# Conv-FFN of a two-layer trunk: the last pair of inner tiles as eight plain block products, and the last weights' loads ahead of the residual's

## The chip, the cores and the metric

The kernel runs on one core of a Trainium2 chip. The metric is the device time of one execution in microseconds (us), lower is better. The kernel before took 2595.81 us as the median of three runs (2591.06 to 2598.98).

The engines are named as in the profile: PE is the matrix engine (TensorE), DVE the vector engine, ACT the scalar engine, POOL the GpSimd engine, and SP the engine that here only issues DMAs. Each works through its own instructions in the order in which they were written.

## The reference, cut to what matters

A residual trunk of two layers (a gated DeltaNet layer and a chunked attention layer) on 1024 tokens of width 1024. Each layer ends in the same kind of feed-forward block, and only that block is changed:

```python
def conv_ffn(xn, w_up, conv_w, conv_b, w_down):
    h = causal_dwconv(xn @ w_up, conv_w) + conv_b      # 1024 x 5632, three taps along the tokens
    gate, val = h[..., :FFN_DIM], h[..., FFN_DIM:]     # FFN_DIM = 2816
    return (jax.nn.silu(gate) * val) @ w_down          # back to 1024 x 1024

h = h + conv_ffn(rmsnorm(h, f_norm[layer]), f_w_up[layer], f_conv[layer], f_conv_b[layer], f_w_down[layer])
```

All matrices are float32, and the last layer is followed by one more RMSNorm.

## The kernel before

`ffn(layer, ...)` (line 1355) makes the block for one layer. The 2816 inner channels are 22 inner tiles of 128 channels (`FP = 22`). Tile j of the gate and tile j of the value belong together: this is a pair j. A pair is a product of a 2 x 2 block matrix of weights with a 2 x 2 block matrix of activations. The block rows of the weights are the gate's 128 channels (operands 11 and 12: inputs 0 to 511 and 512 to 1023) and the value's (21 and 22). The block columns of the activations are the two halves of the tokens (`HALF = 512`).

**Precision.** Every factor is split into a high part and the rest ("hi", "lo"): ACT rounds a copy (`cut_high`, line 1379), and the rest is a subtraction on POOL or DVE (`cut_low`, line 1384). A product of a 128 x 128 weight block with a 128 x 512 activation block is then three matmuls (`triple`, lines 1393 to 1395), and a block product of two 512-deep operands (`product`, line 1509) is four of these, so twelve matmuls of 128x512.

**Seven products instead of eight.** Pairs 1 to 21 are made by a scheme of the Strassen-Winograd kind: seven block products, numbered 1, 7, 6, 5, 2, 4, 3 in the order of the work, on sums and differences of the blocks. The activation sums are made once (`sums`, `X[4]` to `X[7]`); X[5] is the first input half's second token half minus its first. The weight sums are made for every pair on DVE (`left_sum`, line 1444, rows `r<-r,r`), the results are put together on ACT and DVE (`after`, line 1518, tiles `keep`, `keep7`, `gpre`, `vpre`). Pair 0 (`plain`, line 1547) is made with eight plain products. In `after(j, 6)` the sum `keep7` reads the PSUM bank of product 7 before product 4 adds to that bank, so that product 4 waits for DVE there.

**The rest of the pair.** `taps` (line 1476) applies the convolution: its first tap with the bias on ACT (L1485), two more taps on DVE (L1488). Then `silu` on ACT (L1491), `gated` on DVE, and for the last four pairs `hidden` (L1505 on ACT, a subtraction on DVE) splits the result. `w_down` is applied to pairs 0 to 17 in nine groups (`second`, tiles `pd`, `dh`, `eh`), whose results are added up in DRAM by accumulating DMAs from POOL's queue (`send`, L1729, and `send_e`, L1736). The last four pairs go through `tile_of` (layer 1) or `part` (layer 0), tile `pf`, after the last pair. Layer 1's `pf` starts with the residual `res`, loaded by `load_r` (L1872) and transposed by PE.

**Order.** The order of the work is written out: `step` appends a block product to the list `seq`, and `at(i, f, rank)` puts a piece of other work in front of step i. `pos[j, s]` is the place of the s-th product of pair j, and `end` the place of the last one of pair 21. Each engine's order, and SP's order of loads, follows from the order of these calls. For pair 21 there are no group products left between its products, so its seven products follow each other directly.

**Weights' loads.** `load(j, q)` loads operand q of pair j, 256 KB, on SP's queue, under the name `r`. The buffers `r11`, `r21` and `r22` exist twice, `r12` once, so that the load of pair 21's operand 12 waits until that of pair 20 is read. `load_last(q)` (L1779, L1784, tile `fr`) loads the eight pieces of `w_down` for the last four pairs, and `cut_last` splits them (L1790, tiles `fh`, `fl`).

Of the kernel before, what the change touches and what calls it, by code (L numbers as in the profile page):

```python
# [9 lines left out]
F32 = mybir.dt.float32  # L10
# [6 lines left out]
P = 128  # L17
SEQ = 1024
KT = 8
HALF = 512  # L20
NH_A = 8
NH_B = 16
FP = 22
# [5 lines left out]
def trunk_kernel(  # L29
# [1325 lines left out]
    def ffn(layer, h, hp, xs, tail, d_r, last):  # L1355
# [19 lines left out]
        def at(i, f, rank=1):  # L1375

            jobs.setdefault(max(i, 0), []).append((rank, f))
# [9 lines left out]
        def cut(src, ring, copy=nc.scalar.copy):  # L1387
            hi, lo = cut_high(src, ring, copy)
            cut_low(src, hi, lo, nc.gpsimd)
            return hi, lo  # L1390

        def triple(ps, w, x, cw, first, last):
            mm(ps, w[0][:, cw], x[0], start=first, stop=False, skip_group_check=True)  # L1393
            mm(ps, w[0][:, cw], x[1], start=False, stop=False, skip_group_check=True)  # L1394
            mm(ps, w[1][:, cw], x[0], start=False, stop=last, skip_group_check=True)  # L1395
# [80 lines left out]
        def taps(j, v, step, c0=0, c1=SEQ):  # L1476
            w, m = cf[:, layer, FP * v + j, :], FP * v + j
            if (j, v) not in conv_t:
                if v == 0:
                    conv_t[j, v] = tp.tile([P, SEQ], F32, name="gate", tag="gate")  # L1480
                else:
                    conv_t[j, v] = hp.tile([P, SEQ], F32, name="val", tag=f"h{layer + 1}_{j % 4}")
            t_, p_ = conv_t[j, v], pre[j, v]
            if step == 0:
                nc.scalar.activation(t_[:, c0:c1], p_[:, c0:c1], AF.Identity, scale=w[:, 2:3], bias=cfb[:, layer, m : m + 1])  # L1485
            else:
                a = max(c0, step)
                nc.vector.scalar_tensor_tensor(t_[:, a:c1], p_[:, a - step : c1 - step], w[:, 2 - step : 3 - step], t_[:, a:c1], op0=ALU.mult, op1=ALU.add)  # L1488

        def silu(j, c0=0, c1=SEQ):  # L1490
            nc.scalar.activation(conv_t[j, 0][:, c0:c1], conv_t[j, 0][:, c0:c1], AF.Silu)  # L1491

        def gated(j, c0=0, c1=SEQ):
            tt(nc.vector, conv_t[j, 1][:, c0:c1], conv_t[j, 1][:, c0:c1], conv_t[j, 0][:, c0:c1], ALU.mult)

        def hidden(j, c0=0, c1=SEQ):

            if j not in hid:
                if j == FP - 1:
                    hid[j] = [fin.tile([P, SEQ], F32R, name=f"hid{i}", tag=f"hid{i}") for i in "hl"]  # L1500
                else:
                    room_ = {18: (5, 6), 19: (7, 2), 20: (3, 4)}[j]
                    hid[j] = [hp.tile([P, SEQ], F32R, name=f"hid{i}", tag=f"h{layer + 1}_{n}") for n, i in zip(room_, "hl")]
            (hh, hl), v_ = hid[j], conv_t[j, 1]
            nc.scalar.copy(hh[:, c0:c1], v_[:, c0:c1])  # L1505
            tt(nc.vector, hl[:, c0:c1], v_[:, c0:c1], hh[:, c0:c1].bitcast(F32), sub)
# [11 lines left out]
        def after(j, n):  # L1518
            p_ = bank[j, {2: 1, 4: 7, 3: 5}.get(n, n)]
            if n == 1:  # L1520
                keep[j] = tp.tile([P, HALF], F32, name="keep", tag="keep", bufs=2)
                nc.scalar.copy(keep[j], p_)
            elif n == 6:
                tt(nc.vector, keep[j], p_, keep[j], add)
                keep[j, 7] = tp.tile([P, HALF], F32, name="keep7", tag="keep7")
                tt(nc.vector, keep[j, 7], bank[j, 7], keep[j], add)
            elif n == 5:
                tt(nc.vector, new_pre(j, 1)[:, HALF:SEQ], p_, keep[j, 7], add)
            elif n == 2:
                nc.scalar.copy(new_pre(j, 0)[:, 0:HALF], p_)  # L1530
            elif n == 4:
                tt(nc.vector, new_pre(j, 1)[:, 0:HALF], p_, keep[j], add)
            elif n == 3:
                tt(nc.vector, new_pre(j, 0)[:, HALF:SEQ], p_, keep[j], add)

        pos = {}
        ORDER = 1, 2, 5, 3, 6, 7, 4

# [40 lines left out]
        end, fin_at = pos[FP - 1, 7], pos["d", NG - 1, 4]  # L1579
        early = pos["p", 1, 3]  # L1580
        for i, (j, n) in due.items():
            if i < early:
                low = []
                at(i - 2, lambda j=j, n=n, low=low: low.append(operand(j, n, False)), 1)
                at(i - 2, lambda low=low: low[0](), 2.5)
            else:
                at(i - 2, lambda j=j, n=n: operand(j, n), 1)
                if j > 3 and n in (6, 4):
                    at(i - 2, lambda j=j, n=n: left_sum(j, n - 1), 1.05)
            if n != 2 or j > 2:  # L1590
                at(i + 1, lambda j=j, n=n: after(j, n), 0)

        def nx(j, s):
            return pos[j + 1, s] if j + 1 < FP else end + s
# [43 lines left out]


        def half(c0, c1):  # L1640
            return (
                lambda: (taps(FP - 1, 1, 0, c0, c1), taps(FP - 1, 1, 1, c0, c1), taps(FP - 1, 1, 2, c0, c1), taps(FP - 1, 0, 0, c0, c1), taps(FP - 1, 0, 1, c0, c1)),
                lambda: (taps(FP - 1, 0, 2, c0, c1), silu(FP - 1, c0, c1), gated(FP - 1, c0, c1), hidden(FP - 1, c0, c1)),
            )

        def open_fin():
            nonlocal fin
# [116 lines left out]
        k0 = 2 * NG  # L1764
        fw, fh, fps, norms = {}, {}, {}, []
        n0 = len(seq)
        slots = [(k, 1) for k in range(4)] + [(k, 1) for k in range(4, 8)] if layer == 0 else [(k, 0) for k in range(4)] + [(k, 1) for k in range(4)]
        last_at = [pos[FP - 1, s] for s in (3, 4, 5, 6)] + [end + 1] * 4
        if layer == 1:
            last_at = [pos[FP - 1, 2]] + last_at[:-1]  # L1770
            last_at[5] = end
            last_at[7] = end + 2

        def load_last(q):
            tag = ("a11", "a12", "r11", "r21", "r22", "r11", "r22", "r21")[q]
# [16 lines left out]
            fw[q] = hi, lo  # L1792

        for q in range(8):
            s = (1, 1, 2, 3, 4, 4, 5, 6)[q]
            at(fin_at + 1 if q < 2 else pos[FP - 1, s], lambda q=q: load_last(q), 1)
            at(last_at[q], lambda q=q: cut_last(q), 1.5)

        if layer == 0:
# [55 lines left out]
        else:  # L1855
# [645 lines left out]
```

## Time and profile before

| | |
|---|---|
| median of three runs | 2595.81 us (2591.06 to 2598.98) |
| the profiled execution: its own time | 2593.14 us |
| its span, first to last instruction | 2591.4 us |
| mean granted TensorE clock over the span | 0.992 |
| PE busy / DVE / POOL / ACT | 2513.5 / 1856.7 / 1494.1 / 1410.0 us |
| the seven products of pair 21, layer 0 | 1269.34 to 1293.94, 24.60 us |
| the seven products of pair 21, layer 1 | 2505.37 to 2533.05, 27.68 us |

A row of the timeline gives the start in us from the span's start, the duration, the engine, the line of the code, the operation, output and inputs, and shapes; in brackets stands the idle time just before it and who ended it. "PEclk" is the share of the full TensorE clock that was granted. In the table of stretches each engine's busy time stands in the order PE, PEld (PE's weight loads), DVE, ACT, POOL, and behind them PEclk, the busy share of the DMA engines, and GB/s.

### The profile page before, as it was taken

The page shows a single profiled execution, that of the slowest core. Times are in us where ns is not written, and L with a number is a line of the kernel's source. Part 1 is how long each engine was busy: PE and PEld are TensorE (multiplying, and loading weights), DVE is VectorE, ACT ScalarE, POOL GpSimd, SP SyncE. Part 2 cuts the span into 40 slices and gives each one's busy share as a digit, 9 for nine tenths or more (in the row PEclk, how much of TensorE's full clock was granted, in tenths as well). Part 3 has the DMA queues.
Part 4 walks back from the last instruction along what each step waited for, and adds up shares of the span by engine and source line. Part 5 has one row for each costly group of instructions (what it writes and reads, how often), then busy time and mean ns, then how long its engine had stood idle before and what let it go on. Part 6 is the DMA issues. An engine that isn't in the chain of part 4 may idle for free. (4 is left out here: it accounts for less than half of the span.)

```text
span 2591.4 us, 39359 instructions
## 1 busy us (share of the span) xinstructions
PE 2513.5 (97%) x13933; PEld 2078.2 (80%) x13933; DVE 1856.7 (72%) x3102; ACT 1410.0 (54%) x2708; POOL 1494.1 (58%) x1517
## 2 busy tenths in 40 slices
PE   7999999999999999999999999999999999999998
PEld 5878888888777888888778888887876788888877
DVE  5765775454588888888876666666478788888875
ACT  6444555464455656565455556655345556565543
POOL 3655554345447777777735444444443777777771
PEclk9999999999999999999999999999999999999999
DMA  4534345455336777777841111212332577777785
GB/s 128 138 99 121 116 117 164 134 178 169 96 85 143 146 148 154 153 145 153 186 145 48 47 52 57 73 37 73 133 104 78 134 150 143 154 154 153 154 194 175
DMA packets 317061, 325.93 MB, mean 126 GB/s; under 512 B 32832, under 2 KB 240960, under 8 KB 316864
## 3 DMA queue, kind: packets, MB, share of 16 engines
q1 hardware_dynamic: 285728, 219.33, 28.6%
q0 software_dynamic: 26240, 95.43, 20.6%
q10 hardware_dynamic: 4896, 8.65, 0.9%
q8 instruction: 110, 1.80, 0.3%
q14 instruction: 87, 0.71, 0.1%
HBM read 180.68 MB, written 142.67 MB: 125 GB/s over the span
## 5 line engine op out<-in xcount | busy, mean ns | idle before, releaser
L1360 POOL TENSOR_TENSOR ul<-r,uh 128x512 fp32r<-128x512 f32 x282 | 445.6, 1599 | 295.2 <-ACT uh L1381 273.9
L120 PE MATMUL acc<-xh,whi 128*128 128x512 f32 x896 | 375.5, 420 | 0.3 <-ACT xh L1099 0.2
L105 POOL TENSOR_TENSOR wlo<-wraw,whi 128x256 fp32r<-128x256 f32 (+3 forms) x338 | 248.8, 767 | 206.0 <-ACT whi L103 178.1
L122 PE MATMUL acc<-xh,wlo 128*128 128x512 f32 x896 | 353.3, 394 | 4.2 <-POOL wlo L105 4.2
L121 PE MATMUL acc<-xl,whi 128*128 128x512 f32 x896 | 353.4, 394 | 1.3 <-DVE xl L1100 0.8
L1381 ACT CAST uh<-r 128x512 fp32r<-128x512 f32 x296 | 181.7, 623 | 219.8 <-DVE r L1360 175.2
L1395 PE MATMUL pu<-xh,ul 128*128 128x512 f32 x552 | 217.3, 394 | 3.3 <-POOL ul L1360 3.2
L1393 PE MATMUL pu<-xh,uh 128*128 128x512 f32 x552 | 216.7, 393 | 2.9 <-ACT uh L1381 1.4
L1394 PE MATMUL pu<-xl,uh 128*128 128x512 f32 x552 | 216.3, 392 | 1.0 <-POOL xl L381 1.0
L2125 POOL TENSOR_SCALAR sS<-sS,st 128x640 f32<-128x640 f32 (+4 forms) x128 | 86.4, 680 | 206.5 <-DVE st L2123 197.6
L122 PEld LDWEIGHTS acc<-xh,wlo 128*128 128x128 f32 x896 | 168.8, 188 | 42.6 <-POOL wlo L105 5.3
L1714 ACT COPY stage<-pd 128x1024 f32<-128x1024 f32 x180 | 174.8, 1013 | 49.4 <-PE pd L1395 49.4
L121 PEld LDWEIGHTS acc<-xl,whi 128*128 128x128 f32 x896 | 170.0, 190 | 27.8 <-DVE xl L1100 3.1
L120 PEld LDWEIGHTS acc<-xh,whi 128*128 128x128 f32 x896 | 169.7, 189 | 24.5 <-ACT xh L1099 1.2
L1488 DVE SCALAR_TENSOR_TENSOR val<-vpre,colt,val 128x1023 f32<-128x1023 f32 (+2 forms) x92 | 153.6, 1670 | 38.6 <-ACT val L1485 38.4
L2114 DVE CUSTOM_DVE_ANT_0 sS<-sc,bt 128x640 f32<-128x640 f32 (+4 forms) x128 | 84.1, 657 | 132.5 <-PE sc L2110 87.1
L1360 POOL TENSOR_TENSOR dl<-a,dh 128x512 fp32r<-128x512 f32 x90 | 154.8, 1720 | 38.4 <-ACT dh L1381 38.4
L1488 DVE SCALAR_TENSOR_TENSOR gate<-gpre,colt,gate 128x1023 f32<-128x1023 f32 (+2 forms) x92 | 175.4, 1906 | 0.8
L1360 DVE TENSOR_TENSOR r<-r,r 128x512 f32<-128x512 f32 x168 | 131.6, 783 | 31.1 <-POOL ul L1360 29.7
L1395 PEld LDWEIGHTS pu<-xh,ul 128*128 128x128 f32 x552 | 104.3, 189 | 28.0 <-POOL ul L1360 6.6
L1393 PEld LDWEIGHTS pu<-xh,uh 128*128 128x128 f32 x552 | 104.3, 189 | 25.3 <-ACT uh L1381 1.8
L2183 ACT CAST pTh<-ptp 128x512 fp32r<-128x512 f32 (+2 forms) x176 | 75.4, 452 | 89.7 <-PE ptp L2170 86.3
(390 smaller groups left out, 7125.9 us busy)
## 6 DMA issues: line engine op xcount, KB each, us to landing
r<-in_f_w_up_dram SPq DMA_DIRECT2D x172, 256.0 KB, 4.2
d_r<-stage POOLq DMA_DIRECT2D x78, 512.0 KB, 7.9
d_c<-stage POOLq DMA_DIRECT2D x70, 512.0 KB, 7.9
a<-in_f_w_down_dram SPq DMA_DIRECT2D x72, 256.0 KB, 2.8
wraw<-in_a_w_in_dram SPq DMA_DIRECT2D x32, 512.0 KB, 4.7
d_e<-stage POOLq DMA_DIRECT2D x32, 512.0 KB, 9.1
wraw<-in_a_w_out_dram SPq DMA_DIRECT2D x16, 512.0 KB, 4.3
d_r<-h ACTq DMA_DIRECT2D x32, 256.0 KB, 3.6
```

Of the source, the lines that this page charges most:

```text
L105: nc.gpsimd.tensor_tensor(lo[:, c], raw[:, c], hi[:, c].bitcast(F32), op=ALU.subtract)
L120: mm(ps, hi[:, kw, wcol : wcol + P], rh[k][s], start=st, stop=False)
L121: mm(ps, hi[:, kw, wcol : wcol + P], rl[k][s], start=False, stop=False)
L122: mm(ps, lo[:, kw, wcol : wcol + P], rh[k][s], start=False, stop=sp)
L1360: tt = lambda eng, o, a, b, op: eng.tensor_tensor(o, a, b, op=op)
L1381: copy(hi, src)
L1393: mm(ps, w[0][:, cw], x[0], start=first, stop=False, skip_group_check=True)
L1394: mm(ps, w[0][:, cw], x[1], start=False, stop=False, skip_group_check=True)
L1395: mm(ps, w[1][:, cw], x[0], start=False, stop=last, skip_group_check=True)
L1488: nc.vector.scalar_tensor_tensor(t_[:, a:c1], p_[:, a - step : c1 - step], w[:, 2 - step : 3 - step], t_[:, a:c1], op0=ALU.mult, op1=ALU.add)
L1714: nc.scalar.copy(t_, ps)
L2125: nc.gpsimd.tensor_scalar(S, S, st[:, 3:4], 1.0, op0=ALU.mult, op1=ALU.mult)
```

## The change

Pair 21, the last one, is made with eight plain block products and no weight sums. With A1, A2 the two weight blocks of the value (then of the gate), the first token half is A1·X[1] + A2·X[2]. The second token half is A1·X[5] + A2·X[3] plus a copy (`keep`) of A1·X[1], since X[5] is the difference of the two halves. So the products are 21·X1, 21·X5, 22·X2, 22·X3 for the value, then 11·X1, 11·X5, 12·X2, 12·X3 for the gate. Each operand is cut once and used in two products that follow each other. An ACT copy of the bank after the first product (`keep`, L1550 after the change) must be done before the third product adds to the same bank.

The value is finished after the fourth product, so its taps now run in one piece beside the gate's products; the gate is still finished in two halves. The loads of the last weights move ahead by some steps (`load_last`), and in layer 1 the first four tiles' residual loads move back by two steps each (`load_r`); in layer 1 the split pieces of the last weights are also put into other buffers (`slots`, `last_at`).

```diff
+        def plain_operand(q):
+            ops[FP - 1, q] = cut(raw[FP - 1, q], "u")
+
+        def plain_product(q, n):
+            key = "last", q > 20, n in (3, 5)
+            if n in (1, 5):
+                bank[key] = pacc.tile([P, HALF], F32, name="pul", tag="u", bufs=4)
+            for k in range(4):
+                triple(bank[key], ops[FP - 1, q], X[n][k], kc[k], n in (1, 5) and k == 0, n in (2, 3) and k == 3)
+
+        def plain_after(q, n):
+            v, j = q > 20, FP - 1
+            if n == 1:
+                keep[v] = tp.tile([P, HALF], F32, name="keep", tag="keep", bufs=2)
+                nc.scalar.copy(keep[v], bank["last", v, False])
+            elif n == 2:
+                nc.scalar.copy(new_pre(j, int(v))[:, 0:HALF], bank["last", v, False])
+            elif n == 3:
+                tt(nc.vector, new_pre(j, int(v))[:, HALF:SEQ], bank["last", v, True], keep[v], add)
...
-        plan = first + [(j, n) for j in range(3, FP) for n in (1, 7, 6, 5, 2, 4, 3) if (j, n) != (3, 1)]
+        plan = first + [(j, n) for j in range(3, FP - 1) for n in (1, 7, 6, 5, 2, 4, 3) if (j, n) != (3, 1)]
...
+        closing_pair = [(q, n) for v in (20, 10) for q, n in ((v + 1, 1), (v + 1, 5), (v + 2, 2), (v + 2, 3))]
+        for i, (q, n) in enumerate(closing_pair):
+            pos[FP - 1, i + 1] = len(seq)
+            step((FP - 1, q, n), lambda q=q, n=n: plain_product(q, n))
+        pc = [pos[FP - 1, i + 1] for i in range(8)]
...
+        for i, (q, n) in zip(pc, closing_pair):
+            if n in (1, 2):
+                at(i - 2, lambda q=q: plain_operand(q), 1)
+            at(i + 1, lambda q=q, n=n: plain_after(q, n), 0)
...
-        at(end, half(0, HALF)[0], 2)
-        at(end + 1, half(0, HALF)[1], 2)
-        at(end + 2, lambda: (half(HALF, SEQ)[0](), half(HALF, SEQ)[1]()), 2)
+        at(pc[4], lambda: (taps(j_, 1, 0), taps(j_, 1, 1)), 2)
+        at(pc[5], lambda: taps(j_, 1, 2), 2)
+        at(end, lambda: half(0, HALF), 2)
+        at(end + 1, lambda: half(HALF, SEQ), 2)
...
-            s = (1, 1, 2, 3, 4, 4, 5, 6)[q]
-            at(fin_at + 1 if q < 2 else pos[FP - 1, s], lambda q=q: load_last(q), 1)
+            i = (fin_at + 1, fin_at + 1, pos[FP - 2, 6], pos[FP - 2, 7], pc[0], pc[3], pc[1], pc[1])[q]
+            at(i, lambda q=q: load_last(q), 1)
...
-                at(fin_at + 3 + t if t < 4 else end + 1, lambda t=t: load_r(t), 3.5)
+                at(pc[t] if t < 4 else end + 1, lambda t=t: load_r(t), 3.5)
```

What this moves is seen in the built programs. First SP's queue in layer 1, around the load of pair 21's operand 12 (`r_24631` before, `r_24618` after); `stage` is a total that is read back, `res` the residual, `fr` the last weights. Before:

```order
L1733 DMA stage<-d_e_1_19578 128x1024
L1872 DMA res<-d_r_97 128x4x128
L1872 DMA res<-d_r_99 128x4x128
L1439 DMA r_24631<-in_f_w_up_dram 128x4x128
L1872 DMA res<-d_r_97 128x4x128
L1872 DMA res<-d_r_99 128x4x128
```

After the change:

```order
L1766 DMA stage<-d_e_1_19570 128x1024
L1813 DMA fr<-in_f_w_down_dram 128x512 x2
L1439 DMA r_24618<-in_f_w_up_dram 128x4x128
L1813 DMA fr<-in_f_w_down_dram 128x512
L1901 DMA res<-d_r_97 128x4x128
L1901 DMA res<-d_r_99 128x4x128
```

Two loads still stand ahead of the operand's, but they are last weights and no longer residual.

Then the same place in layer 0, where there is no residual to load. Before:

```order
L1733 DMA stage<-d_e_1_7524 128x1024
L1439 DMA r_12572<-in_f_w_up_dram 128x4x128
L1779 DMA fr<-in_f_w_down_dram 128x4x128 x6
L1843 DMA h_12755<-d_r_89 128x512
L1843 DMA h_12756<-d_r_89 128x512
```

After the change:

```order
L1766 DMA stage<-d_e_1_7524 128x1024
L1808 DMA fr<-in_f_w_down_dram 128x4x128 x2
L1439 DMA r_12571<-in_f_w_up_dram 128x4x128
L1808 DMA fr<-in_f_w_down_dram 128x4x128 x4
L1872 DMA h_12757<-d_r_89 128x512
```

In layer 0 operand 12 was next after the total, and now two last weights' loads of 256 KB stand ahead of it.

Last ACT in layer 1, beside the gate's products; `gate<-gate` is pair 20's silu, `uh` the high part of an operand. Before, from the cut of the operand for pair 21's product 2 on (`r_24631`):

```order
L1381 CAST uh<-r_24631 128x512
L1790 CAST fh_24717<-fr 128x512
L1505 CAST hidh<-val 128x1024
L1381 CAST uh<-r_24560 128x512
L1790 CAST fh_24751<-fr 128x512
L1491 ACTIVATE gate<-gate 128x1024
```

After the change, from the copy of the value's first half on:

```order
L1552 COPY vpre<-pul 128x512
L1819 CAST fh_24729<-fr 128x512
L1491 ACTIVATE gate<-gate 128x1024
L1381 CAST uh<-r_24618 128x512
L1485 ACTIVATE val<-vpre,colt 128x1024
L1550 COPY keep<-pul 128x512
```

Operand 12's cut now stands behind pair 20's silu, and the copy `keep`, for which the seventh product waits, stands behind that cut and the value's first tap.

More of the change, by code (lines that the diff above doesn't have):

```diff
@@ L1578, in ffn @@
                         step(("d", g, n), lambda g=g, n=n: second(g, n))
-        end, fin_at = pos[FP - 1, 7], pos["d", NG - 1, 4]
+        closing_pair = [(q, n) for v in (20, 10) for q, n in ((v + 1, 1), (v + 1, 5), (v + 2, 2), (v + 2, 3))]
[3 more added lines that the diff above has]
+        pc = [pos[FP - 1, i + 1] for i in range(8)]
+        end, fin_at = pc[7], pos["d", NG - 1, 4]
         early = pos["p", 1, 3]
@@ L1591, in ffn @@
                 at(i + 1, lambda j=j, n=n: after(j, n), 0)
+        j_ = FP - 1
+        for i, (q, n) in zip(pc, closing_pair):
+            if n in (1, 2):
+                at(i - 2, lambda q=q: plain_operand(q), 1)
+            at(i + 1, lambda q=q, n=n: plain_after(q, n), 0)
         def nx(j, s):
@@ L1640, in half @@
         def half(c0, c1):
[L1641 to L1644, printed above, removed]
+            for i in range(3):
+                taps(j_, 0, i, c0, c1)
+            silu(j_, c0, c1)
+            gated(j_, c0, c1)
+            hidden(j_, c0, c1)
         def open_fin():
@@ L1766, in ffn @@
         n0 = len(seq)
[L1767 to L1772, printed above, removed]
+        slots = [(k, 1) for k in range(4)] + [(k, 1) for k in range(4, 8)] if layer == 0 else [(k, 1) for k in range(4)] + [(k, 0) for k in range(4)]
+        last_at = pc[:4] + ([end + 1] * 4 if layer == 0 else [pc[5], pc[6], end, end + 1])
         def load_last(q):
```

## The prediction

> **What bounds the kernel now.** I read the page's busy times first, then the stretches of pair 21 in both layers, then PE's timeline inside them, then the chain of waits that leads to each idle time there.
>
> ```profile
> PE 2513.5 (97%) x13933; PEld 2078.2 (80%) x13933; DVE 1856.7 (72%) x3102; ACT 1410.0 (54%) x2708; POOL 1494.1 (58%) x1517
> ```
>
> PE is busy for 97% of the span, so elsewhere one more matmul costs its own time and work taken off DVE, ACT or POOL brings nothing. The change is at pair 21, so the question is whether that holds there.
>
> ```profile
> 1269.34:1293.94 24.60, 21.21 (x85) 16.75 (x84) 20.99 (x17) 11.69 (x17) 13.61 (x9) 0.93 0.81 195
> 2505.37:2533.05 27.68, 23.32 (x86) 17.65 (x85) 22.39 (x19) 13.00 (x20) 14.54 (x10) 0.88 0.95 247
> 2533.05:2584.77 51.72, 51.72 (x257) 42.19 (x255) 30.15 (x50) 18.71 (x35) 1.73 (x2) 1.00 0.53 174
> ...
> 1287.55:1290.96 3.41, 3.41 (x9) 2.62 (x8) 2.75 (x3) 1.92 (x4) 2.70 (x2) 0.50 0.78 195
> 2519.76:2523.17 3.41, 3.23 (x8) 2.56 (x9) 3.14 (x2) 1.38 (x3) 3.41 (x3) 0.50 1.12 329
> ```
>
> It does not: in the first two stretches, the seven products of pair 21 in layers 0 and 1, PE has idle time and less than the full clock (PEclk 0.93 and 0.88), while DVE is nearly full. In the third, the last stage of layer 1, PE never stops. The last two rows are pieces of the first two in which the clock was granted at one half. PE's timeline shows the causes; first layer 0, the first matmul of the products 1, 5, 2, 4 and 3 and of the next stage (`pf`):
>
> ```profile
> 1269.34 0.39 PE L1393 MATMUL pu<-xh,uh 128*128 128x512 f32 x1
> ...
> 1277.50 0.39 PE L1393 MATMUL pu<-xt1h,uh 128*128 128x512 f32 x1
> 1280.54 0.39 PE L1393 MATMUL pu<-xh,uh 128*128 128x512 f32 x1
> 1286.78 0.47 PE L1393 MATMUL pu<-xt4h,uh 128*128 128x512 f32 x1 [3.36 <-DVE keep L1360]
> 1291.20 0.39 PE L1393 MATMUL pu<-xh,uh 128*128 128x512 f32 x1
> 1293.94 0.39 PE L1393 MATMUL pf<-hidh,fh 128*128 128x512 f32 x1
> ```
>
> The first three products take 8.16 us, so 2.72 each, with no wait. Seven would be 19.04; the stretch is 24.60, an excess of 5.56: 0.32 in the fourth product, 3.52 in the fifth up to the end of the wait for `keep7` (3.36 idle), 1.70 in the sixth, which runs at half clock right behind that wait, 0.02 in the last. Layer 1:
>
> ```profile
> 2505.37 0.39 PE L1393 MATMUL pu<-xh,uh 128*128 128x512 f32 x1
> ...
> 2510.81 0.39 PE L1393 MATMUL pu<-xt2h,uh 128*128 128x512 f32 x1
> 2511.85 0.50 PE L1395 MATMUL pu<-xt2h,ul 128*128 128x512 f32 x1 [0.42 <-POOL ul L1360]
> 2514.29 0.39 PE L1393 MATMUL pu<-xt1h,uh 128*128 128x512 f32 x1
> 2518.58 0.50 PE L1393 MATMUL pu<-xh,uh 128*128 128x512 f32 x1 [1.41 <-ACT uh L1381]
> 2519.94 0.79 PE L1395 MATMUL pu<-xh,ul 128*128 128x512 f32 x1 [0.62 <-POOL ul L1360]
> 2525.89 0.47 PE L1393 MATMUL pu<-xt4h,uh 128*128 128x512 f32 x1 [1.90 <-DVE keep L1360]
> 2533.05 0.60 PE L1886 MATMUL pf<-ident,res 128*128 128x128 f32 x4
> ```
>
> Here the excess over 19.04 is 8.64: 0.76 in the third product (a wait for POOL), 1.57 in the fourth and 4.59 in the fifth (three waits, 3.93 idle, and some 2 at half clock), 1.72 in the last two at half clock. The chain of waits of layer 1 says what was late:
>
> ```profile
> 2501.76 16.05 DMA r<-in_f_w_up_dram
> 2518.44 0.62 ACT fh L1790
> ...
> 2520.03 2.17 DVE hidl L1360
> ...
> 2524.42 0.61 DVE keep L1360
> ```
>
> The load of operand 12, which product 2 needs as fifth, takes 16.05 us; ACT stands still for it, and with ACT DVE's queue, down to `keep7`. In layer 0 DVE alone is late with `keep7`.
>
> **The change part by part.** *The eighth product* costs 2.72 us of PE in each layer, 5.44 together, on the path. *The waits for `keep7`* go, since no product adds to a bank that DVE still has to read. *Operand 12* is needed as the seventh product, 16.32 us after the start of the first instead of 10.88 plus waits, so layer 1's wait for it goes, with its half clock. With no wait the eight products take 21.76 in either layer.
>
> *The wait in the third product of layer 1* I keep:
>
> ```profile
> 2509.60 0.87 POOL L1736 DMA_DIRECT2D d_c<-stage  x1 [3.30 <-DMA d_c<-stage]
> 2510.21 1.59 POOL L1360 TENSOR_TENSOR ul<-r,uh 128x512 fp32r<-128x512 f32 x1
> ```
>
> POOL issues an accumulating DMA that waits 3.30 us for an earlier one, and the low part of the third product's operand stands behind it. After the change operand 22 stands there. Bounds 0 and 0.76; I take 0.76, as nothing moves that DMA.
>
> So layer 0 gains 24.60 - 21.76 = 2.84, layer 1 gains 27.68 - 21.76 - 0.76 = 5.16.
>
> *DVE, ACT and POOL* lose three operand cuts, three weight sums and the two `keep` sums per layer, which counts only through the waits above. What is added there is the copy `keep` on ACT: the seventh product waits for it. Its queue, by rows of layer 0:
>
> ```profile
> 1271.88 1.41 DVE L1360 TENSOR_TENSOR r<-r,r 128x512 f32<-128x512 f32 x2
> 1274.26 1.47 DVE L1360 TENSOR_TENSOR hidl<-val,hidh 128x1024 fp32r<-128x1024 f32 x1 [0.97 <-ACT hidh L1505]
> ...
> 1279.09 1.78 DVE L1360 TENSOR_TENSOR fl<-fr,fh 128x512 fp32r<-128x512 f32 x1
> ...
> 1283.03 2.28 DVE L1488 SCALAR_TENSOR_TENSOR gate<-gpre,colt,gate 128x1022 f32<-128x1022 f32 x1
> ```
>
> ```profile
> 1268.80 1.24 ACT L1485 ACTIVATE val<-vpre,colt 128x1024 f32<-128x1024 f32 x1
> 1275.28 0.57 ACT L1522 COPY keep<-pu 128x512 f32<-128x512 f32 x1
> 1278.77 0.62 ACT L1790 CAST fh<-fr 128x512 fp32r<-128x512 f32 x1
> 1285.41 1.06 ACT L1491 ACTIVATE gate<-gate 128x1024 f32<-128x1024 f32 x1 [6.02 <-DVE gate L1488]
> ```
>
> On ACT stand ahead of the copy pair 20's silu (1.06), the cut of operand 12 (0.62, as the other casts), the value's first tap (1.24) and the copy itself (0.57), some 3.2 with their overlap. The seventh product starts at 1269.34 + 16.32 = 1285.66, so DVE's last tap of pair 20's gate must end by about 1282.4. Before it ended at 1285.3. Ahead of it go two sums (1.41), the idle 0.97, and about 1.2 at the queue's head (one more sum and a cast that ACT had to make first); one cut of last weights (0.7 to 1.78) comes in; and POOL has one subtraction less beside it, where each one lengthens a tap from 1.3 to 2.3. That gives 1281.2 to 1282.3: in time, by 0.1 to 1.2. I take no wait; the other end, with POOL's help left out, is 1 us late.
>
> *The loads.* In layer 1 two loads of 256 KB stand ahead of operand 12's as before, so by the 16.05 it lands no later than 2517.8; the cut must start by 2505.37 + 16.32 - 2.2 = 2519.5. In layer 0 it was the first in the queue and becomes the third:
>
> ```profile
> 1265.53 0.37 SPq L1439 DMA_DIRECT2D r<-in_f_w_up_dram  x1
> ...
> r<-in_f_w_up_dram SPq DMA_DIRECT2D x1, 256.0 KB, 10.0
> ...
> fr<-in_f_w_down_dram SPq DMA_DIRECT2D x2, 256.0 KB, 15.5
> fr<-in_f_w_down_dram SPq DMA_DIRECT2D x1, 256.0 KB, 2.8
> ...
> 2517.83 1.20 SPq L1872 DMA_DIRECT2D res<-d_r  x2
> ```
>
> As first it took 10.0 us and landed at 1275.6. The second and third there, issued within two microseconds behind it, took 15.5, so landed by about 1282.2; a single one issued once the accumulating DMAs were over took 2.8. Third place is thus 1282.2, and the cut may start as late as 1285.66 - 2.2 = 1283.4. Bounds 1275.6 and, at 10.0 for each of the three, 1295.5; I take 1282.2, the row of that very place in the queue, so no cost. The residual's first four tiles in layer 1 are issued two steps, 5.4 us, later. The last pair of these loads was issued at 2517.83 (the last row), so now at about 2523.3; at the 2.8 of a free queue it lands at 2526, and the transposes behind the last product need the first tile from 2527.9 on and this fourth one last. I cost that at nothing: the last products cover it, and without them it would cost its lateness, one for one.
>
> *The end of each layer* has less behind the last product than before, as the value is finished by then; before it hid under the next stage's matmuls, 51.72 busy of 51.72 in layer 1. No cost, no gain. In layer 0 one wait stands further down:
>
> ```profile
> 1332.25 1.05 PE L372 MATMUL pss<-ones,nacc 128*128 128x2 f32 x8 [1.43 <-DVE nacc L369]
> ```
>
> It is the norm behind the block, late on DVE. With less DVE work ahead it may go, or stay: 0 to 1.43, I take 0.7.
>
> The sum: 2.84 + 5.16 + 0.7 = 8.7 us. Against the profiled execution's own 2593.14 (span 2591.4) that is 2584.4; its run lies 2.7 below the median of 2595.81, from which it would be 2587.1. I take 2586, between the two.
>
> **The rivals.** *The half clock does not hang on these waits.* For it: layer 1's idle times are short, 1.41, 0.62 and 1.90, and yet a window is 3.41 long (2519.76 to 2523.17). Then 1.70 in layer 0 and about 3.7 in layer 1 stay: a gain of 3.3, 2591.4. Against it: each half-clock window begins inside or right behind a wait, and the stretch with PE busy without a break has PEclk 1.00. The Trainium skill, "TensorE: Matmul & The Clock Gate", section "Why this matters for your kernels", holds that the clock falls back after an idle window and warns of gaps over some 3 us between matmuls. By that rule layer 0's 3.36 would do it and layer 1's gaps would not, so that only layer 1's 3.7 would stay, 2589.7. This trace speaks against so long a threshold: 0.50 was granted around waits of under 2 us.
>
> *The copy `keep` is late.* Each layer where it is 2 us late pays 2 and 1.7 of half clock: 2589.7 with one, 2593.4 with both. For it: a margin of 0.1 to 1.2 on DVE and 1.2 on the load.
>
> *The other side: operand 12 of layer 0 stuck behind the last weights.* At 10.0 us for each load it lands at 1295.5, PE waits 12.1 at the seventh product and runs 1.7 longer behind it: 2586 + 13.8 = 2599.8, slower than before. It turns the gain into a loss from a landing at about 1290.4 on. Against it: third place took 15.5 us, not 30.
>
> **How the numbers follow.** The forecast has 0.60, the late copy 0.22 (mostly one layer), the half clock that stays 0.10, the stuck operand 0.08. A measurement of this kernel tells about 0.3%, 7.8 us, from no change. The forecast's 8.7 lies little above: of its 0.60 I put 0.52 beyond 7.8, plus 0.10 from the late copy where it is only tenths late and layer 1's third wait goes too. Faster 0.62. The rest of the rivals on this side is within 0.3%, 0.32; of the stuck operand 0.06 is slower by more. The range: at the low end every wait gone, the third product's and the norm's too (8.76 + 1.43 = 10.2, from 2593.14: 2583), and 3 us for the spread of the runs; at the high end the copy late in both layers. 2580 to 2593.5.
>
> **What would show it.** Right: the eight products take 21.8 in layer 0 and 21.8 to 22.5 in layer 1, PEclk 1.00 in both, no wait for `keep`, and operand 12 of layer 0 landing near 1282 and cut in time. Wrong: a wait of the seventh product's first matmul for ACT `keep`, or ACT standing before the cut of operand 12 for a DMA, with a half-clock window behind it; or half clock without a wait.

## The result and the profile after

The changed kernel took 2583.89 us (median of 7 runs, 2581.55 to 2590.04), the kernel before beside it 2594.50 (median of 7): a ratio of 0.9967, 95% interval 0.9955 to 0.9980, so about 8.6 us less. The profiled execution of the changed kernel has a span of 2582.2, that of before 2591.4.

The page's line of busy times, and then the windows of the changed kernel: pair 21 of layer 0, pair 21 of layer 1, and the last stage of layer 1. Columns are length, then busy time (and instructions) of PE, PEld, DVE, ACT and POOL, PEclk, DMA share, GB/s.

```profile
PE 2510.3 (97%) x13957; PEld 2076.1 (80%) x13957; DVE 1845.4 (71%) x3084; ACT 1409.3 (55%) x2704; POOL 1483.3 (57%) x1511
```

```profile
1270.95:1293.12 22.17, 22.11 (x97) 17.94 (x96) 20.24 (x16) 12.42 (x17) 7.85 (x6) 1.00 0.89 219
2501.32:2523.79 22.47, 22.32 (x98) 17.82 (x97) 20.51 (x16) 13.59 (x20) 9.22 (x7) 1.00 1.09 277
2523.79:2575.51 51.72, 51.72 (x257) 42.17 (x255) 26.80 (x46) 16.44 (x32) 1.29 (x1) 1.00 0.55 184
```

Eight products take 22.17 and 22.47 us where seven took 24.60 and 27.68, at full clock (1.00, before 0.93 and 0.88); PE is busy in 22.11 and 22.32 of them. The last stage is the same 51.72. PE's timeline shows the starts of the first and seventh product and of the next stage in layer 0, the same three in layer 1, and the norm's matmul behind layer 0:

```profile
1270.95 0.39 PE L1393 MATMUL pul<-xh,uh 128*128 128x512 f32 x1
...
1287.55 0.50 PE L1393 MATMUL pul<-xh,uh 128*128 128x512 f32 x1
...
1293.12 0.39 PE L1393 MATMUL pf<-hidh,fh 128*128 128x512 f32 x1
...
1330.63 1.05 PE L372 MATMUL pss<-ones,nacc 128*128 128x2 f32 x8 [0.63 <-DVE nacc L369]
...
2501.32 0.39 PE L1393 MATMUL pul<-xh,uh 128*128 128x512 f32 x1
...
2518.20 0.50 PE L1393 MATMUL pul<-xh,uh 128*128 128x512 f32 x1
...
2523.78 0.38 PE L1915 MATMUL pf<-ident,res 128*128 128x128 f32 x2
```

The seventh product starts 16.60 us behind the first in layer 0 and 16.88 in layer 1; six products without a wait are 16.32. What holds it is in the waits of layer 1's stretch, where PEld is the weight load ahead of a matmul:

```profile
POOL d_c L1769 <- DMA d_c<-stage: 4.4, 1, 4.4
...
PEld pul L1393 <- ACT keep L1550: 0.6, 1, 0.6
PEld pul L1395 <- POOL ul L1360: 0.4, 1, 0.4
```

The copy `keep` is a little late, and so is GpSimd's low part of operand 22, for the third product, which stands behind an accumulating DMA. The norm's wait fell from 1.43 to 0.63. Together: 24.60 - 22.17 = 2.43, 27.68 - 22.47 = 5.21, and 0.80, which makes 8.44 of the profiled span's 9.2. The other 0.8 is the rest of larger differences in stretches that the change does not touch: this execution comes to pair 21 of layer 0 1.61 us later than that of before, and takes 2.43 us less from the norm to pair 21 of layer 1, where one window ran at half clock and before five.

### The profile page after: what moved, and what is told of

The parts are those of the page before. It is cut to its first block, busy times and chain, and to the rows that moved or that the text cites. A ratio compares the mean times of both kernels' runs of the same rounds, so it can differ in the third digit from the quotient of the medians.

```text
span 2582.2 us, 39356 instructions
## 1 busy us (share of the span) xinstructions
PE 2510.3 (97%) x13957; PEld 2076.1 (80%) x13957; DVE 1845.4 (71%) x3084; ACT 1409.3 (55%) x2704; POOL 1483.3 (57%) x1511
## 5 line engine op out<-in xcount | busy, mean ns | idle before, releaser
L1360 POOL TENSOR_TENSOR ul<-r,uh 128x512 fp32r<-128x512 f32 x276 | 437.4, 1605 | 286.4 <-ACT uh L1381 265.2
L1395 PE MATMUL pu<-xh,ul 128*128 128x512 f32 x528 | 207.0, 392 | 2.7 <-POOL ul L1360 2.6
L1393 PE MATMUL pu<-xh,uh 128*128 128x512 f32 x528 | 206.6, 391 | 1.4 <-DVE h L1261 0.9
L1394 PE MATMUL pu<-xl,uh 128*128 128x512 f32 x528 | 206.4, 391 | 1.0 <-POOL xl L381 1.0
L1488 DVE SCALAR_TENSOR_TENSOR val<-vpre,colt,val 128x1023 f32<-128x1023 f32 x88 | 152.9, 1738 | 35.6 <-ACT val L1485 35.6
L1360 DVE TENSOR_TENSOR r<-r,r 128x512 f32<-128x512 f32 x160 | 126.3, 789 | 31.1 <-POOL ul L1360 29.7
L1360 DVE TENSOR_TENSOR el<-val,eh 128x512 fp32r<-128x512 f32 x90 | 86.3, 959 | 46.0 <-ACT eh L1381 46.0
```

The lines of the kernel that those rows point to most:

```text
L1360: tt = lambda eng, o, a, b, op: eng.tensor_tensor(o, a, b, op=op)
```

## Experiments

**The changed kernel once more**, beside the next three.

> The changed kernel itself, to compare the others with on the same chip: about 2584 us, 8 to 10 less than the kernel before, stretches of 22.2 and 22.5 us.

2585.45 us beside 2591.32, ratio 0.9973 (0.9962 to 0.9985), somewhat less than the 8 to 10 us expected; its stretches are 22.46 and 23.28. In layer 1 the third product waits 1.22 us for GpSimd here, so that wait differs from execution to execution. Against the same profile of before, the two stretches of this execution gain 2.14 and 4.40 us.

**Products without the loads' order.** The cuts of the first last weights go back with their loads.

```diff
-        last_at = pc[:4] + ([end + 1] * 4 if layer == 0 else [pc[5], pc[6], end, end + 1])
+        last_at = [pc[2], pc[3], pc[4], pc[5]] + [end + 1] * 4 if layer == 0 else [pc[1], pc[2], pc[3], pc[4], pc[5], end, end + 1, end + 2]
...
-            i = (fin_at + 1, fin_at + 1, pos[FP - 2, 6], pos[FP - 2, 7], pc[0], pc[3], pc[1], pc[1])[q]
+            i = (fin_at + 1, fin_at + 1, pc[1], pc[2], pc[3], pc[3], pc[4], pc[5])[q]
...
-                at(pc[t] if t < 4 else end + 1, lambda t=t: load_r(t), 3.5)
+                at(fin_at + 3 + t if t < 4 else end + 1, lambda t=t: load_r(t), 3.5)
```

> The eight plain products stand, but the loads of the last weights, the cuts they feed and the first loads of the residual are issued where they were before the change. Theory one: the gain comes from the products, because the accumulating product no longer waits for the two sums keep and keep7, and the order of the loads carries nothing. Then layer 0 takes 21.8 to 22.4 us in the eight products, layer 1 22.0 to 23.0, the clock stays at 1.00, and the whole is within 2 us of the changed kernel (about 2584). Rival: layer 1 needs the loads' order too. Then the last weights come in behind the residual's tiles, ScalarE stands still for them ahead of the copy keep, and layer 1 takes 25 us or more, with half clock behind a wait: about 2587.

2589.87 us, ratio 0.9991 (0.9982 to 1.0000): nearly all the gain is gone. The windows of both stretches, then from the timelines of layer 1 PE's seventh product, ScalarE's cut of the third last weight, SyncE's loads, and SyncE's own waits at the residual's:

```profile
1266.40:1288.16 21.76, 21.76 (x98) 18.02 (x96) 18.78 (x16) 12.54 (x17) 9.50 (x6) 1.00 0.94 230
2497.70:2527.30 29.60, 24.72 (x98) 19.64 (x97) 20.53 (x16) 13.45 (x19) 9.24 (x7) 0.88 1.07 307
```

```profile
2519.31 0.80 PE L1393 MATMUL pul<-xh,uh 128*128 128x512 f32 x1 [4.88 <-ACT keep L1550]
...
2514.62 0.62 ACT L1819 CAST fh<-fr 128x512 fp32r<-128x512 f32 x1 [7.68 <-DMA fr<-in_f_w_down_dram]
...
2494.47 12.77 SPq L1901 DMA_DIRECT2D res<-d_r  x4
2507.29 2.63 SPq L1813 DMA_DIRECT2D fr<-in_f_w_down_dram  x1
...
SPq L1901 <- PE pul L1395: 6.9, 2, 6.6
```

In layer 0 the products alone do it all: 21.76, eight times 2.72 without a wait. In layer 1 they are worse than before, 29.60 against 27.68. SyncE stands 12.77 us at four of the residual's loads, 6.9 of it until PE has read the buffers that they fill; the last weight's load comes behind them, ScalarE waits 7.68 us for it, and the copy `keep`, further back on ScalarE, keeps PE waiting 4.88. The first theory is wrong for layer 1, the rival right.

**The loads' order without the products**, on the kernel before.

```diff
-            s = (1, 1, 2, 3, 4, 4, 5, 6)[q]
-            at(fin_at + 1 if q < 2 else pos[FP - 1, s], lambda q=q: load_last(q), 1)
+            i = (fin_at + 1, fin_at + 1, pos[FP - 2, 6], pos[FP - 2, 7], pos[FP - 1, 1], pos[FP - 1, 4], pos[FP - 1, 5], pos[FP - 1, 6])[q]
+            at(i, lambda q=q: load_last(q), 1)
...
-                at(fin_at + 3 + t if t < 4 else end + 1, lambda t=t: load_r(t), 3.5)
+                at(pos[FP - 1, t + 1] if t < 4 else end + 1, lambda t=t: load_r(t), 3.5)
```

> The kernel before, seven products with their sums, with only the loads issued in the new order (last weights ahead of the residual's first tiles; two of the last weights stay where they were, since their rooms are still in use). Theory one: nothing is gained. Layer 0 stays at 24.6 us (its waits are on VectorE's queue), layer 1 at 26.5 to 28, the whole within 2 us of the kernel before. Rival: the order of the loads is what took layer 1's waits away. Then layer 1 falls to 24.5 us or less and the whole by 3 us or more.

2596.94 us, ratio 1.0018 (1.0009 to 1.0027): slower. The windows, and a wait in layer 0:

```profile
1270.83:1297.83 27.00, 21.96 (x86) 16.52 (x84) 20.07 (x17) 11.78 (x17) 13.62 (x9) 0.94 0.69 166
2509.35:2536.62 27.27, 23.40 (x85) 17.58 (x84) 22.39 (x19) 12.94 (x20) 14.58 (x10) 0.87 1.02 252
```

```profile
ACT uh L1381 <- DMA r<-in_f_w_up_dram: 5.5, 1, 5.5
```

Layer 0 loses 2.40, because operand 12, now third in the queue, is still needed as fifth and ScalarE waits 5.5 us for it; layer 1 gains 0.41. The theory had layer 0 unmoved and missed that; that the loads alone bring no gain holds. The parts don't add: in layer 1 the products alone cost 1.92, the loads alone bring 0.41, and both together bring 5.21.

**Which load it is in layer 1.** Once the products without the loads' order, but with the residual at the changed places, and once the changed kernel with only the residual at the old places (each is the last pair of lines of the first diff, one way or the other).

> The eight products with the last weights' loads and cuts at the old places, as in products_alone, but the residual's first four tiles loaded at the changed kernel's places, each one or two products later. In products_alone SyncE stood 12.77 us at the residual's third to sixth load, and the last weights' third load, issued behind them at 2507.29, kept ScalarE 7.68 us. Theory: that stand is the cause, so with the residual behind the third load ScalarE's wait falls under 3 us, keep is late by less than 2 us, and layer 1 takes 22.0 to 25 us, not 29.60. Rival: the last weights' own late places are the cause; then ScalarE still waits some 7 us for the third load and layer 1 stays at 28 us or more. Layer 0 has no residual loads and stays at 21.8 to 22.2 by both.

> The changed kernel with only the residual's first four tiles loaded at the old places. The last weights' third and fourth load are now issued ahead of the residual's load at which SyncE stands. Theory: what matters is that these two are not behind that stand, so the residual's place alone does nothing: layer 1 takes 22.0 to 23.5 us, as the changed kernel's 22.47 and 23.28. Rival: the residual's place itself counts, since its loads share the transfers with operand 12; then operand 12 or a last weight lands late, and layer 1 takes 25 us or more.

Layer 1's stretch in the first, with ScalarE's first wait for a last weight, and in the second:

```profile
2498.35:2524.01 25.66, 23.71 (x98) 19.06 (x97) 18.62 (x16) 13.56 (x19) 10.80 (x7) 0.93 1.08 297
...
2511.44 0.62 ACT L1819 CAST fh<-fr 128x512 fp32r<-128x512 f32 x1 [4.09 <-DMA fr<-in_f_w_down_dram]
```

```profile
2501.00:2523.02 22.02, 22.02 (x97) 17.89 (x96) 19.66 (x15) 11.66 (x16) 8.02 (x6) 1.00 1.09 279
```

(One run each, 2584.11 and 2583.13 beside 2588.60.) Putting the residual back at its old places does no harm as long as the last weights keep their new ones: 22.02. Moving the residual alone halves the excess over 21.76 but leaves 4.09 us of ScalarE's wait and 25.66, between what the theory and the rival expected. What counts most is that the last weights are issued early, ahead of the loads at which SyncE stands; ScalarE's longest waits are for the third of them. Their cuts were moved along with their loads, so whether later cuts alone would have done it is not shown.

**Why `keep` was late in the changed kernel.** DVE's first tap of pair 20's gate in layer 0 of the changed kernel, with GpSimd's subtractions at that time, and then the same tap with the cuts of last weights later:

```profile
1275.17 5.03 DVE L1488 SCALAR_TENSOR_TENSOR gate<-gpre,colt,gate 128x1023 f32<-128x1023 f32 x1
...
1275.00 1.62 POOL L1360 TENSOR_TENSOR ul<-r,uh 128x512 fp32r<-128x512 f32 x1
1276.38 1.49 POOL L1360 TENSOR_TENSOR fl<-fr,fh 128x512 fp32r<-128x512 f32 x1
1277.63 1.48 POOL L1360 TENSOR_TENSOR ul<-r,uh 128x512 fp32r<-128x512 f32 x1
```

```diff
-        last_at = pc[:4] + ([end + 1] * 4 if layer == 0 else [pc[5], pc[6], end, end + 1])
+        last_at = [pc[5], pc[6], end, end] + [end + 1] * 4 if layer == 0 else [pc[2], pc[3], pc[5], pc[5], pc[6], pc[6], end, end + 1]
```

> The changed kernel with the cuts of the first four last weights 3 to 5 products later, so that fewer subtractions stand on GpSimd and VectorE ahead of pair 20's gate. Theory: the first VectorE tap of pair 20's gate, 5.03 and 5.31 us in the changed kernel, is held by three GpSimd subtractions run back to back; with two it takes about 3.5, everything behind it on VectorE is 2 to 4 us earlier, the copy keep is ready before the seventh product, and the eight products take 21.8 us in layer 0 and 22.0 in layer 1: 0.5 to 1 us less in all. Rival: the lateness of keep is set by the load of operand 12 or by the products themselves; then the stretches stay at 22.2 and 22.5. Against both: the later cuts could be late for the first matmuls of the next stage, which would show as a wait there.

```profile
1270.49 1.27 DVE L1488 SCALAR_TENSOR_TENSOR gate<-gpre,colt,gate 128x1023 f32<-128x1023 f32 x1
...
1266.87:1288.97 22.10, 22.06 (x98) 17.95 (x97) 17.25 (x15) 12.43 (x17) 8.43 (x6) 1.00 0.90 218
2503.05:2525.86 22.81, 22.05 (x97) 17.90 (x96) 17.49 (x15) 12.69 (x19) 7.88 (x7) 1.00 1.09 274
```

The tap takes 1.27, less than the 3.5 expected, since it now starts ahead of GpSimd's subtractions (the first at 1271.20), and no wait for `keep` is left. The whole, 2584.77 us, ratio 0.9965 (0.9952 to 0.9979), is not told from the changed kernel's, and the stretches miss the 21.8 and 22.0 expected: the third product's wait for GpSimd stays, 0.76 in layer 1. So next that operand's low part was made on VectorE, with the later cuts kept:

```diff
-            ops[FP - 1, q] = cut(raw[FP - 1, q], "u")
+            ops[FP - 1, q] = hi, lo = cut_high(raw[FP - 1, q], "u")
+            cut_low(raw[FP - 1, q], hi, lo, nc.vector if q == 22 else nc.gpsimd)
```

> The changed kernel with the later cuts of the run before (first four last weights) and the low part of operand 22, which the third product needs, made on VectorE and not on GpSimd, where it stands behind an accumulating DMA that waits 4.4 to 4.7 us for an earlier one. Theory: that was the last wait in the eight products, so they take 21.8 us in both layers, 1.1 less in all than with the later cuts alone; the rest is the same. Rival: the subtraction is late on VectorE too, or holds a tap there so that keep or the gate is late; then a wait of the same size shows at another product.

```profile
1268.38:1290.14 21.76, 21.76 (x97) 18.02 (x96) 17.43 (x16) 12.43 (x17) 6.10 (x5) 1.00 0.99 235
2498.50:2520.27 21.77, 21.77 (x98) 17.97 (x97) 17.28 (x17) 13.34 (x20) 7.61 (x6) 1.00 1.10 275
```

No wait is left: 21.76 and 21.77. 2581.14 us, ratio 0.9954 (0.9941 to 0.9966), the lowest measured, though its interval overlaps the changed kernel's.

**Is it the form of the products?** The kernel before with its seven products, and with what stood ahead of `keep7` and of operand 12 moved instead (the added lines):

```diff
+                when[j].append(({18: fin_at + 5, 19: fin_at + 9}.get(j, nx(j, 6)), (hidden,), 1.9))
...
+        p6 = pos[FP - 1, 6]
+        last_at = [p6, end, end, end] + [end + 1] * 4 if layer == 0 else [p6, p6, end, end, end, end, end + 1, end + 2]
...
+            s = (1, 1, 2, 3, 4, 4, 5, 6)[q] if layer == 0 else (0, 0, 1, 1, 1, 4, 5, 6)[q]
+            at(pos[FP - 2, 7] if s == 0 else fin_at + 1 if q < 2 else pos[FP - 1, s], lambda q=q: load_last(q), 1 if s else 3.2)
...
+                at(pos[FP - 1, (1, 2, 6, 6)[t]] if t < 4 else end + 1, lambda t=t: load_r(t), 3.5)
```

> The kernel before, still seven products for pair 21 with their sums, but with what delays keep7 and operand 12 moved: the cuts of the first last weights stand two to five products later, the low part of pair 19's hidden value two later, and in layer 1 the load of operand 12 goes ahead of the last weights and of the residual, of which the third and fourth tile go three or four products later. Theory: seven products cost 19.04 us and the loss was in what stood ahead of them on ScalarE, VectorE and SyncE, not in the form of the products; without it layer 0 takes 19.4 to 20.5 us and layer 1 19.8 to 21.5, at clock 1.00, and the whole is 11 to 13 us less than the kernel before, 3 to 5 less than the changed one. Rival: keep7 is late by VectorE's own sums and taps, whatever the cuts; then a wait of 1.5 us or more stays in each layer with half clock behind it, and the whole is no better than the changed kernel.

2589.16 us, ratio 0.9982 (0.9972 to 0.9991). The two stretches, and PE's waits in the stages behind them:

```profile
1268.92:1288.33 19.41, 19.33 (x85) 15.69 (x84) 16.04 (x15) 10.17 (x15) 10.60 (x7) 1.00 0.94 229
2504.60:2524.28 19.68, 19.38 (x85) 15.64 (x84) 16.48 (x15) 10.72 (x16) 12.67 (x8) 1.00 1.08 280
```

```profile
PE pf L1393 <- DVE gpre L1360: 2.4, 1, 2.4
...
PE pf L1888 <- DVE fl L1360: 2.6, 2, 1.9
```

The seven products run without their waits, 19.41 and 19.68, so the loss before was in the queues and not in the products. The whole fell far short of the 11 to 13 us: the work that was put off now stands in front of the next stage, 2.4 and 2.6 us of waiting with half clock behind. A second arrangement, again from the kernel before (the lines that differ from the first one; `hidden_high` and `hidden_low` are the parts of `hidden` on ScalarE and VectorE):

```diff
+                    when[j] += [(fin_at + 7, (hidden_high,), 1.9), (fin_at + 9, (hidden_low,), 1.4)]
...
-        at(end, half(0, HALF)[0], 2)
+        at(end + 1, half(0, HALF)[0], 1.9)
...
+        last_at = [p6, end, end, end] + [end + 1] * 4 if layer == 0 else [p5, p5, p6, end, p6, end, end + 1, end + 2]
...
+            cut_low(fw[q], hi, lo, nc.gpsimd if q % 2 and (layer, q) != (1, 3) else nc.vector)
```

> The seven products of seven_clean, whose stretches took 19.4 and 19.7 us, but with the work behind them set right: pair 21's last sum, which frees a bank for the next stage, goes ahead of the first taps of its halves on VectorE; in layer 1 three cuts of last weights are one or two products earlier and the low part of the fourth is on VectorE; ScalarE's half of pair 19's hidden value is back at its old place. Theory: the waits of 2.40 us in layer 0's last stage and of 1.86 and 0.71 in layer 1's, each with a half-clock window behind it, were what ate the gain, so they go, the stretches stay at 19.4 and 19.7, and the whole is 13 us less than the kernel before, 3 to 5 less than the changed kernel. Rival: VectorE has too much to do there in any order; then the waits come back at another place, of 2 us or more, and the whole stays within 3 us of the changed kernel.

```profile
1269.44:1288.83 19.39, 19.36 (x86) 15.69 (x84) 17.06 (x16) 10.50 (x15) 11.30 (x7) 1.00 0.91 217
2500.39:2519.82 19.43, 19.41 (x86) 15.65 (x84) 17.62 (x15) 10.65 (x16) 13.04 (x8) 1.00 1.08 279
...
1323.20 0.50 PE L1393 MATMUL pf<-hidh,fh 128*128 128x512 f32 x1 [1.57 <-DVE h L1360]
```

2581.28 us, ratio 0.9963 (0.9951 to 0.9976). The waits right behind the products are gone but for 0.2 us; one of 1.57 comes up further down in layer 0. Its stretches are 2.8 and 3.0 us shorter than the changed kernel's. That the whole is 3 to 5 less than the changed kernel's was expected and is not shown: the interval covers both that and no difference. The 13 us less than before that were expected lie just outside it. Seven products rearranged and eight products tuned (0.9954) are not told apart, so the gain does not need the plain form.

**When the clock halves.** The copy `keep` was repeated, so that the seventh product waits by a set amount.

```diff
-                nc.scalar.copy(keep[v], bank["last", v, False])
+                for _ in range(1 if v else (3, 5)[layer]):
+                    nc.scalar.copy(keep[v], bank["last", v, False])
```

> The changed kernel with the copy keep of the gate made three times in layer 0 and five times in layer 1, one after the other on ScalarE (the same copy, the result is the same), so that the seventh product waits some 1.6 us in layer 0 and 2.8 in layer 1. By the forecast, that half clock follows any wait of over about 1.4 us, a half-clock window of 3.41 us stands in both stretches: 22.2 + 1.1 + 1.7 = 25.0 us and 22.5 + 2.2 + 1.7 = 26.4. By the rival, and by the rule of the Trainium skill that only a gap of some 3 us does it (TensorE: Matmul & The Clock Gate, Why this matters for your kernels), the clock stays at 1.00 in both: 23.3 and 24.7.

The stretches, the wait in layer 1, and the two 3.41 us windows of the clock in which that wait lies:

```profile
1264.75:1288.44 23.69, 22.31 (x97) 17.86 (x96) 20.60 (x16) 13.59 (x19) 7.89 (x6) 1.00 0.91 226
2498.98:2524.17 25.19, 22.43 (x98) 17.82 (x96) 22.25 (x17) 16.21 (x24) 9.69 (x7) 1.00 1.08 286
...
2514.00:2517.41 3.41, 1.97 (x9) 1.31 (x7) 2.96 (x2) 3.31 (x6) 1.81 (x1) 1.00 1.18 304
2517.41:2520.83 3.42, 2.28 (x10) 1.87 (x11) 1.53 (x2) 3.04 (x5) 0.27 (x1) 1.00 1.07 322
```

```profile
2518.55 0.50 PE L1393 MATMUL pul<-xh,uh 128*128 128x512 f32 x1 [2.58 <-ACT keep L1551]
```

Waits of 1.38 and 2.58 us, and the clock stays at 1.00. That is against what the expectation took from the forecast, that any wait of over about 1.4 us halves the clock. (One run, 2584.28.) With a longer wait in layer 1, and in layer 0 operand 12's load put back:

```diff
+                for _ in range(1 if v else (1, 9)[layer]):
...
+                at(pc[1] if (layer, j, q) == (0, FP - 2, 12) else pos[j, s], lambda j=j, q=q: load(j + 1, q), 3)
```

> The changed kernel with the copy keep made nine times in layer 1, and in layer 0 the load of operand 12 issued two products later, behind five loads of last weights and not two. Layer 1: a wait of about 5 us at the seventh product, and by the forecast and the rival alike a half-clock window behind it: 22.5 + 4.5 + 1.7 = 28.7 us. Layer 0, by the forecast's row (third place took 15.5 us, whatever stands ahead): it lands some 16 us after its issue, near 15 to 17 us into the stretch, and the products take 24 to 27 us. By the rival, in which each load ahead costs 3 us or more, it lands 6 us or more later than that and the products take 33 us or more.

```profile
2502.75:2530.74 27.99, 23.49 (x98) 18.95 (x97) 21.88 (x17) 18.56 (x28) 11.93 (x7) 0.94 1.08 301
2519.91:2523.33 3.42, 0.00 (x0) 0.00 (x0) 0.20 (x1) 3.23 (x7) 0.00 (x0) 1.00 1.09 320
2523.33:2526.74 3.41, 3.01 (x7) 2.43 (x8) 2.25 (x3) 2.33 (x4) 1.00 (x1) 0.50 1.04 371
...
1277.62 0.59 SPq L1439 DMA_DIRECT2D r<-in_f_w_up_dram  x1
...
1284.39 0.62 ACT L1381 CAST uh<-r 128x512 fp32r<-128x512 f32 x1 [1.96 <-DMA r<-in_f_w_up_dram]
...
1269.51:1292.29 22.78, 22.09 (x97) 17.94 (x96) 18.46 (x16) 12.54 (x17) 8.71 (x6) 1.00 0.87 215
```

(One run, 2590.85.) The wait of 4.50 us empties a whole window, and the next is at half. Shorter ones do it too where they fall into one window; here is the wait of 1.95 us in the run with the residual late, and a window of the kernel before with two waits in it, each with the window that follows:

```profile
2514.53:2517.94 3.41, 1.46 (x7) 0.98 (x6) 1.64 (x2) 3.19 (x5) 2.34 (x2) 1.00 1.12 330
2517.94:2521.35 3.41, 3.41 (x10) 2.66 (x9) 3.03 (x4) 0.58 (x1) 0.00 (x0) 0.50 1.04 391
```

```profile
2516.35:2519.76 3.41, 1.56 (x6) 0.66 (x4) 0.58 (x1) 1.85 (x3) 1.15 (x1) 1.00 1.09 299
2519.76:2523.17 3.41, 3.23 (x8) 2.56 (x9) 3.14 (x2) 1.38 (x3) 3.41 (x3) 0.50 1.12 329
```

PE idle for 1.95 and for 1.85 us of one window was followed by half clock; 2.58 us, split into 1.44 and 1.14 by a border, was not. Layer 0 of this kernel is in the last section.

## Why the prediction was right, step by step

- **The eighth product at 2.72 us**: right. Without waits eight take 21.76 us (products alone, layer 0; the tuned version, both layers).
- **The waits for `keep7` go**: right. No product waits for VectorE, and layer 0 gains this by either order of the loads.
- **Layer 1's 5.16** came out at 5.21, but for a reason that the prediction did not have. It put the gain down to operand 12's later need. That wait does go with the products alone (ScalarE cuts operand 12 at 2516.10 without standing for it), but another comes in its place. Of the loads it said that the residual's later place costs nothing, which holds (the last stage starts without a wait), but the earlier place of the last weights had no term at all: that is the step that failed. Without the new order of the loads and their cuts layer 1 takes 29.60 and not 22.47, so the order is worth 7.1 us there, all of it hidden in the words "With no wait". That the sum still met 5.21 so closely is in part luck: the third product's wait came 0.5 shorter than its term and the late copy, which had none, took about as much. The runs show the last weights behind SyncE's stand, the third above all (7.68 us), and not operand 12, as what would have been late.
- **The copy `keep` in time by 0.1 to 1.2 us**: missed by little. The seventh product started 0.28 and 0.56 us later than 16.32, of which the third product's wait had taken 0.05 and 0.25 before. That is the rival of the late copy at tenths of a microsecond, with no half clock behind it. The term that was off is VectorE's: "one subtraction less" beside a tap was taken to save time, while three in a row held one tap for 5.03 us.
- **Operand 12 third in layer 0's queue**: right; with 16.5 us from issue (1267.09) to landing it came 12.6 us into the stretch, forecast 12.9, and ScalarE cut it without a wait.
- **The third product of layer 1 at 0.76, the norm at 0.7**: 0.25 and 1.22 in two executions of the changed kernel and 0.76 with the later cuts; the norm gave 0.80.
- **The half clock**: the windows went, as forecast, since no long wait was left. The rival that it does not hang on these waits is wrong, and so is the reading, drawn from the forecast, that any wait of 1.4 us or so does it. The forecast's doubt about a threshold of 3 us was right: 1.95 us did it.

The sum was 8.7; the same three terms measured make 8.44.

## What to carry to other kernels

A load's place in a queue has to be priced by what stands behind it when the queue itself stops: here 12.77 us at loads whose buffers were not free made a load late which an in-order engine then waited for, and that decided the sign of the change in one layer. Where a change has two parts, each may be worth nothing or less alone, so do not give the gain to one of them without a run of that part. And before paying a matmul product for a wait, see what stands in front of the late instruction: seven products ran in 19.4 us once cuts and loads were moved, though the work must then not land in front of the next stage.

## What the runs showed of the hardware

The clock goes by fixed windows. In the kernel before, half-clock windows begin at 1287.55 and 2519.76; the distance, 1232.21, is 361 times 3.4133 us, and each window lasts 3.41. In each of the thirteen profiled executions all half-clock windows begin on such a grid, to 0.005 us. If PE is idle for about half of a window, the next can run at half clock: idle times of 1.85, 1.95 and 3.42 in a window did it, 1.44 and 1.14 did not. Over the thirteen executions, their first 30 us left out, no window with over 1.94 us of idle PE was followed by full clock (worked out from PE's rows, window by window). From 1.50 to 1.93 us it went either way: of such full-clock windows 30 were followed by half clock and 32 were not. Below 1.50 it was rare, four windows with 0.90 to 1.14 us of idle PE. So idle time alone is not the whole rule, and what else counts stays open. The windows do not start with the kernel: in two executions of the changed kernel half-clock windows begin at 677.72 and 675.69, 2.03 us apart and so not on one grid. So the same wait can cost 1.7 us more in one execution and nothing in another, which also makes executions differ. The Trainium skill, "TensorE: Matmul & The Clock Gate", section "Part 1: The HAM clock gate (the "warmup" mystery)", has the free-running window of 3413 ns, and the trace agrees; its rule of gaps over some 3 us (section "Why this matters for your kernels") allows too much here, where 1.95 us within one window did it; 2.58 us across a border did not, as the rule has it.

A VectorE operation can be held by several GpSimd subtractions in a row: 5.03 us against 1.27 alone, with the three subtractions beginning 1.38 and 1.25 us apart as if VectorE were not there. The Trainium skill, "SBUF — State Buffer", section "SBUF: two separate sides", says that a VectorE operation with two inputs in SBUF and a reading GpSimd operation lock each other out for a whole instruction; that the loser can lose three times running is what this trace adds.

A load issued late need not land late. In the last kernel above operand 12 of layer 0 was issued 8.1 us into the stretch, 12 us later than in the changed kernel, and ScalarE had it 6.8 us after the issue; in the changed kernel it took 16.5 us. The stretch was 22.78 us, better than both expectations (one run), and the stuck operand, the rival on the other side, is the less likely for it.
